# Gathering page keys through copied row lists, with a pause taken out and two sets of rooms

## The chip, the cores and the metric

The kernel runs on one core of one Trainium2 chip. The metric is the device time of one execution in microseconds (us). The core has five instruction queues that run beside each other, each strictly in its own order: TensorE (PE, matmuls; PEld is its loading of weights), VectorE (DVE), ScalarE (ACT), GpSimd (POOL) and SyncE (SP, which only issues DMA transfers here). POOL issues the indirect DMA transfers, the gathers.

## The reference, cut to what matters

One decoder layer for 1024 prompt tokens and for 8 sequences of 4 new tokens. The part that the change touches is the attention of the new tokens over 8192 past tokens, whose latent keys (256 wide) and rotary keys (64 wide) lie in pages of 128 tokens, found through a page table:

```python
def one_seq(args):
    ql, qr, pt, c_new, r_new = args
    c_past = cache_ckv[pt].reshape(-1, KV_LORA)
    r_past = cache_kr[pt].reshape(-1, MLA_ROPE)
    s_past = jnp.einsum('thc,kc->htk', ql, c_past) + jnp.einsum('thr,kr->htk', qr, r_past)
    ...
    p = jax.nn.softmax(sc, axis=-1).astype(c_new.dtype)
    return (jnp.einsum('htk,kc->thc', p[..., :n_past], c_past)
            + jnp.einsum('htk,kc->thc', p[..., n_past:], c_new))
```

Beside it the layer has input projections (x times w_in, in many columns), a retention branch, the attention of the prompt, gates and output projections. All values are float32.

## The kernel before, in words

**Matmuls in parts.** The projections split each float32 operand in a high and a low half and run three matmuls for each product (lines 266 to 268, helper mac). Each weight tile is loaded by SP, cast by ACT (line 247) and its low half taken by DVE (line 198). One weight tile of a gate or value column serves 72 matmuls of 128x352.

**Fill.** The columns of w_in that belong to gates and to the retention values are computed by a generator called `fill`, which gives way after each product. Three stages consume it, each through `beside(main, total, fill, budget)`: after each step of the stage's own work, which yields a cost, as many products of fill are issued as the budget allows in proportion. What is left of fill runs by itself at the end (`run(fill)`, line 717). The yields of the stage thus set how many fill matmuls stand between its steps.

**Page attention** (lines 576 to 703). The eight sequences go in two groups g of four. In each group the 64 pages of a sequence go in eight steps jj of eight pages. One pair (g, jj), a unit, is one run of `past_keys`: sixteen units in all, here numbered 0 to 15. Of a unit:

- `gather` issues, for each of four sequences s and each of two blocks i, one indirect DMA of the rotary keys (128 rows of 1 KB, line 584, tile rraw) and one of the latent keys (128 rows of 4 KB, line 585, tile craw). The row numbers lie in the columns of `idx`, worked out once before (`page_rows`).
- Five steps n make scores. Step 0 takes the rotary keys, steps 1 to 4 take 64 columns each of the latent keys. In each, DVE turns the keys of the four sequences (line 634, tile kt, a ring of 8, so two steps' worth), and PE runs 32 score matmuls (line 640).
- DVE takes the maximum (line 645, nb), ACT the exponentials (line 652), PE turns the probabilities (line 661), DVE and ACT copy them out (line 662), PE multiplies them with the latent keys (line 667, pv), and DVE adds that to the running sum (line 669, acc).

The tile craw has 8 rooms, two units' worth; rraw has 2 rooms of two sequences each, one unit's worth. A tile's new writer waits for all readers of the room's last content.

**Order.** A scheduler in the tile layer puts the instructions on each engine's queue: it follows the program, but lets an instruction that it takes to be ready earlier go ahead of others. So the order on DVE is not that of the source: the turned rotary keys of the next unit, for one, stand ahead of the maximum of this one. What stands in a queue behind a waiting instruction waits too.

Of the kernel before, what the change touches and what calls it, by code (L numbers as in the profile page):

```python
# [9 lines left out]
F32 = mybir.dt.float32  # L10
F32R = mybir.dt.float32r
BF16 = mybir.dt.bfloat16
I32 = mybir.dt.int32
# [6 lines left out]
P = 128  # L20
# [4 lines left out]
NR = NB * NS  # L25
# [4 lines left out]
NPG = PAST // PAGE  # L30
# [3 lines left out]
HM = 8  # L34
NOPE = 128
ROPE = 64
QL = 384
KL = 256
# [122 lines left out]
def decode_step(ctx: ExitStack, tc: tile.TileContext, A: dict, O: dict):  # L161
    nc = tc.nc
    pe, act, dve, pool, sp = nc.tensor, nc.scalar, nc.vector, nc.gpsimd, nc.sync
# [207 lines left out]
    idx = lp.tile([P, NB * NPG // 4], I32, name="idx")  # L371
# [102 lines left out]
    p3 = ph.enter_context(tc.tile_pool(name="p3", bufs=1))  # L474
    NSEQ, NJ, NK = 4, 10, 2

    def big(name, shape, rows_=P):
        return p3.tile([rows_, *shape], F32, tag="craw", name=name, bufs=2 * NSEQ)

    def mid(name, shape):  # L480
        return p3.tile([P, *shape], F32, tag="mid", name=name, bufs=2)
# [14 lines left out]
    def sample_queries():  # L496
        pt = tr()
        for i in range(5):
            pe.transpose(pt[:, i * NR:(i + 1) * NR], latS[:, i * P:(i + 1) * P], ident[:NR, :NR])
        pe.transpose(pt[:ROPE, 5 * NR:6 * NR], latS[:, QL + KL:], ident[:NR, :NR])  # L500
        cqT = p3.tile([P, 3, NR], F32, name="cqT")
        dve.tensor_copy(cqT, pt[:, :3 * NR].rearrange("p (a b) -> p a b", a=3))
        dve.tensor_copy(kvST, pt[:, 3 * NR:5 * NR].rearrange("p (a b) -> p a b", a=2))
        dve.tensor_copy(krST, pt[:ROPE, 5 * NR:6 * NR])
        wq = [big("wq", (3, 384)) for _ in range(4)]
        for c in range(4):
            sp.dma_start(wq[c], A["w_uq"][0, :, c * 384:(c + 1) * 384].rearrange("(k p) f -> p k f", p=P))
        wk = big("wk", (2, HM, NOPE))
        for c in range(2):
            sp.dma_start(wk[:, c], A["w_ukv"][0, c * P:(c + 1) * P, :].rearrange("p (h d) -> p h d", h=HM)[:, :, :NOPE])  # L510
        yield 6.0
        qs = big("qq", (1536,))[:NR].rearrange("p (h d) -> p h d", h=HM)
        qq = big("qq", (768,))
        qr = qq[:NR, :512].rearrange("p (h d) -> p h d", h=HM)
        qnT = qq[:, 512:768].rearrange("p (h r) -> p h r", h=HM)
        ps = mm()
        for k in range(3):
            for c in range(4):
                pe.matmul(ps[c * NR:(c + 1) * NR, :384], cqT[:, k, :], wq[c][:, k], start=k == 0,
                          stop=k == 2, tile_position=(0, c * NR), skip_group_check=True)  # L520
        yield 2.0
        for c in range(4):
            act.activation(qs[:, 2 * c:2 * c + 2, :].rearrange("p h d -> p (h d)"), ps[c * NR:(c + 1) * NR, :384], AF.Copy, scale=MSC)  # L523
            yield 0.5
        for c in range(2):
            rope_nat(qr[:, 4 * c:4 * c + 4, :], qs[:, 4 * c:4 * c + 4, NOPE:], 8, NR, p3, 4, "qro")
            yield 1.0
        pt = tr()
        for h in range(HM):
            pe.transpose(pt[:, h * NR:(h + 1) * NR], qs[:, h, :NOPE], ident[:NR, :NR])  # L530
        act.copy(qnT, pt[:, :HM * NR].rearrange("p (h r) -> p h r", h=HM))
        yield 1.0
        wkT = big("wkT", (HM, KL))
        for h in range(HM):
            pt = tr()
            for c in range(2):
                pe.transpose(pt[:, c * P:(c + 1) * P], wk[:, c, h, :], ident)
            (act.copy if h % 2 else dve.tensor_copy)(wkT[:, h, :], pt[:, :KL])
            yield 0.5
        qlT = Q["qlT"] = ring("qlT", (2, NB, 32))  # L540
        pl = mm()
        for c in range(2):
            for h in range(HM):
                o = (c * HM + h) * NR
                pe.matmul(pl[:, o:o + NR], wkT[:, h, c * P:(c + 1) * P], qnT[:, h, :], start=True, stop=True)
            dve.tensor_copy(qlT[:, c].rearrange("p b (h t) -> p h b t", t=NS),
                            pl[:, c * HM * NR:(c + 1) * HM * NR].rearrange("p (h b t) -> p h b t", h=HM, b=NB))
            yield 2.0
        pt = tr()
        for h in range(HM):  # L550
            pe.transpose(pt[:ROPE, h * NR:(h + 1) * NR], qr[:, h, :], ident[:NR, :NR])
        dve.tensor_copy(qrT.rearrange("p b (h t) -> p h b t", t=NS), pt[:ROPE, :HM * NR].rearrange("p (h b t) -> p h b t", h=HM, b=NB))
        sel = ring("sel", (4, 4, 32))
        dve.tensor_copy(sel, ident.rearrange("p (q r) -> p q r", q=4).unsqueeze(2).to_broadcast([P, 4, 4, 32]))
        sel = sel.rearrange("p q g r -> p q (g r)")
        q4 = q4_tile()
        other = [ring("q4b", (w, NSEQ, 32)) for w in (4, 4, 2)]
        for n in range(5):
            px = tr()
            for i in range(2):  # L560
                j = 2 * n + i
                o = px[:, i * 256:(i + 1) * 256]
                if j < 8:
                    pe.matmul(o, sel[:, j % 4], qlT[:, j // 4].rearrange("p b r -> p (b r)"), start=True, stop=True)
                else:
                    pe.matmul(o, sel[:ROPE, i], qrT.rearrange("p b r -> p (b r)"), start=True, stop=True)
            src = px.rearrange("p (i g s r) -> p i g s r", i=2, g=2, s=NSEQ)
            dve.tensor_copy(q4[:, 2 * n:2 * n + 2], src[:, :, 0])
            act.copy(other[n // 2][:, 2 * (n % 2):2 * (n % 2) + 2], src[:, :, 1])
            yield 1.0  # L570
        for n, o in enumerate(other):
            w = 4 if n < 2 else 2
            sp.dma_start(q4D[:, 4 * n:4 * n + w], o)
        Q["q4"] = q4
# [1 line left out]
    rows_c = A["cache_ckv"].rearrange("l n (s a) c -> (l n s) (a c)", a=4)  # L576
    rows_r = A["cache_krope"].rearrange("l n (s a) c -> (l n s) (a c)", a=4)

    def gather(b, jj, c, r):

        for i in range(NK):
            at_ = b * (NPG // 4) + NK * jj + i
            off = bass.IndirectOffsetOnAxis(ap=idx[:, at_:at_ + 1], axis=0)
            pool.indirect_dma_start(out=r[:, i], out_offset=None, in_=rows_r, in_offset=off)  # L584
            pool.indirect_dma_start(out=c[:, i], out_offset=None, in_=rows_c, in_offset=off)  # L585

    def new_tokens(g, st):

# [20 lines left out]
        act.copy(acc, pv[:, :KL])  # L609
        yield 1.0  # L610

    def past_keys(g, jj, st):

        seqs = [4 * g + s for s in range(NSEQ)]
        rr = [p3.tile([P, 2, NK, 4 * ROPE], F32, tag="rr", name="rraw", bufs=2) for _ in range(2)]
        cr = [big("craw", (NK, 4 * KL)) for _ in seqs]  # L620
        for s, b in enumerate(seqs):
            gather(b, jj, cr[s], rr[s // 2][:, s % 2])
        keys = [c.rearrange("p i (a d) -> p (i a) d", a=4) for c in cr]
        rope = [rr[s // 2][:, s % 2].rearrange("p i (a d) -> p (i a) d", a=4) for s in range(NSEQ)]
        yield 6.0
        W = 128 * NK
        sc = psg.tile([P, 4, 512], F32, tag="sc", name="sc", bufs=1)[:, :, :W]
        steps = [8, *range(0, 8, 2)]
        for n, j in enumerate(steps):
            kt = []  # L630
            for s in range(NSEQ):
                t = ring("kt").rearrange("p (j k) -> p j k", j=2)
                src = keys[s][:, :, 32 * j:32 * j + 64] if j < 8 else rope[s]
                dve.transpose(t.rearrange("p j (n r) -> p n j r", r=32), src.rearrange("p n (j r) -> p n j r", r=32))  # L634
                kt.append(t)
            for i in range(2):
                for q in range(4):
                    qs_ = slice(32 * q, 32 * q + 32)
                    for s in range(NSEQ):
                        pe.matmul(sc[32 * s:32 * s + 32, q, :], Q["q4"][qs_, j + i, s, :], kt[s][qs_, i, :], start=n + i == 0,  # L640
                                  stop=n == NJ // 2 - 1 and i == 1, tile_position=(32 * q, 32 * s), skip_group_check=True)
            if n % 2:
                yield 6.0
# [21 lines left out]
        for n in range(4 * NK):  # L665
            for s in range(NSEQ):
                pe.matmul(pv[32 * s:32 * s + 32, :KL], pT[:, n, 32 * s:32 * s + 32], keys[s][:, n, :], start=n == 0, stop=n == 4 * NK - 1,  # L667
                          tile_position=(0, 32 * s), skip_group_check=True)
        dve.scalar_tensor_tensor(out=acc, in0=acc, scalar=corr, in1=pv[:, :KL], op0=ALU.mult, op1=ALU.add)
        yield 1.0  # L670

    def page_attention():
        state = [{}, {}]
        yield from new_tokens(0, state[0])
        for g in range(2):
            if g == 1:
                q4 = q4_tile()
                sp.dma_start(q4, q4D)
                Q["q4"] = q4
                yield from new_tokens(1, state[1])  # L680
            for jj in range(NPG // 4 // NK):
                yield from past_keys(g, jj, state[g])
        olT = ring("olT", (2, HM, NB, NS))
        for g, st in enumerate(state):
            rl = p3.tile([P, 1], F32, tag="rl", name="rl", bufs=2)
# [274 lines left out]
    for h in range(HR):  # L960
        run(head_vg(h, X))
        nxt = {}
# [521 lines left out]
```

## Time and profile before

| | |
|---|---|
| median of 3 runs | 2253.39 us (2249.23 to 2253.68) |
| the profiled execution | 2248.48 us, of it span 2246.7 us |
| PE busy | 2192.1 us |
| DVE busy | 1207.9 us |
| ACT busy | 709.8 us |
| POOL busy | 509.9 us |
| score matmuls (line 640) | from 207.6 to 791 us of the span |
| gathers (lines 584 and 585) | 128 and 128, 123.7 and 120.5 us of POOL |

A row of a timeline gives the start in the span, the duration, the engine, the line and operation, the tiles (out<-in), their shapes, and xN for N instructions merged; in square brackets stands the engine's idle time before the row and what ended it. A score matmul leaves two records. Time to landing is from a transfer's issue to its data's arrival.

### The profile page before, as it was taken

How to read it: one execution, taken by the hardware profiler on the slowest of the kernel's cores; microseconds unless marked ns; L12 is line 12 of the kernel's file. 1: busy time of each engine (PE TensorE's matmuls, PEld its weight loads, DVE VectorE, ACT ScalarE, POOL GpSimd, SP SyncE). 2: the span in 40 equal slices, each digit the busy share in tenths (PEclk: the TensorE clock that was granted, in tenths of full speed). 3: DMA queues.
4: the chain of work that ended last, by engine and by line, in shares of the span. 5: the costliest groups of instructions: out<-in, count | busy, mean ns of one | idle time of the engine just before them, and what ended most of it. 6: DMA issues, size and time to landing. Idle time of an engine off the chain costs nothing.

```text
span 2246.7 us, 45040 instructions
## 1 busy us (share of the span) xinstructions
PE 2192.1 (98%) x18482; PEld 1975.0 (88%) x18482; DVE 1207.9 (54%) x2624; ACT 709.8 (32%) x1532; POOL 509.9 (23%) x682
## 2 busy tenths in 40 slices
PE   8899999999999999999999999999999999999997
PEld 7898888888888899798798779888887999999997
DVE  5414454444544438728638447767767344454465
ACT  6312112222322123222222122355456332222243
POOL 2224434344444114203203102122222000000021
PEclk9999999999999999999999999999999999999999
DMA  8446565656565442532613753200110453333243
GB/s 234 131 148 247 184 223 174 227 183 222 182 232 178 153 135 59 165 99 66 212 49 95 237 162 87 81 23 24 37 46 27 149 192 106 96 94 107 87 141 114
DMA packets 293391, 303.65 MB, mean 135 GB/s; under 512 B 29760, under 2 KB 242048, under 8 KB 293184
## 3 DMA queue, kind: packets, MB, share of 16 engines
q1 hardware_dynamic: 268608, 216.86, 31.3%
q0 software_dynamic: 24576, 83.90, 10.8%
q8 instruction: 145, 2.38, 0.4%
q14 instruction: 62, 0.51, 0.1%
HBM read 234.76 MB, written 65.94 MB: 134 GB/s over the span
## 4 chain that ended last, share of the span: by engine, by line
PE 82%; DVE 7%; issue 6%; POOL 3%; ACT 2%; DMA 1%; SPq 0%; POOLq 0%; ACTq 0%; DVEq 0%
PE mm L266 19%; PE mm L268 18%; PE mm L267 18%; PE sc L640 5%; PE x L667 3%; PE mm L1199 2%; PE ac L267 2%; PE ac L268 2%; PE ac L266 2%; PE tr L1186 1%; PE ac L936 1%; PE ac L932 1%; DVE Stl L198 1%; PE ac L1139 1%; PE tr L791 1%
## 5 line engine op out<-in xcount | busy, mean ns | idle before, releaser
L266 PE MATMUL mm<-xh,wh 128*128 128x352 f32 x1728 | 577.4, 334 | 0.2 <-ACT qq L523 0.2
L268 PE MATMUL mm<-xh,wl 128*128 128x352 f32 x1728 | 562.4, 325 | 0.0
L267 PE MATMUL mm<-xl,wh 128*128 128x352 f32 x1728 | 560.5, 324 | 0.0
L266 PEld LDWEIGHTS mm<-xh,wh 128*128 128x128 f32 x1728 | 324.6, 188 | 38.4 <-issue 29.5
L268 PEld LDWEIGHTS mm<-xh,wl 128*128 128x128 f32 x1728 | 325.5, 188 | 18.6 <-issue 17.3
L267 PEld LDWEIGHTS mm<-xl,wh 128*128 128x128 f32 x1728 | 325.8, 189 | 14.5 <-issue 7.2
L198 DVE TENSOR_TENSOR wl<-wr,wh 128x512 fp32r<-128x512 f32 (+2 forms) x283 | 189.0, 679 | 202.4 <-ACT wh L247 175.7
L247 ACT CAST wh<-wr 128x512 fp32r<-128x512 f32 x248 | 149.8, 619 | 356.0 <-PE mm L267 319.2
L634 DVE STREAM_TRANSPOSE kt<-craw 128x512 f32<-128x512 f32 x256 | 159.3, 679 | 151.0 <-PE sc L640 150.4
L413 ACT ACTIVATE gev<-mm 128x352 f32<-128x352 f32 x132 | 61.1, 463 | 357.2 <-PE mm L268 256.7
L584 POOL DMA_INDIRECT rraw<-in_cache_krope_dram,idx x128 | 123.7, 966 | 215.4 <-DVE kt L634 166.2
L585 POOL DMA_INDIRECT craw<-in_cache_ckv_dram,idx x128 | 120.5, 941 | 142.6 <-PE x L667 102.2
L640 PE MATMUL sc<-kt,q 32*32 32x256 f32 x5120 | 125.5, 385 | 0.1
L266 PE MATMUL mm<-mh,wh 128*128 128x352 f32 x384 | 124.3, 324 | 0.8 <-DVE M L1309 0.8
L267 PE MATMUL mm<-ml,wh 128*128 128x352 f32 x384 | 124.5, 324 | 0.0
L268 PE MATMUL mm<-gh,wl 128*128 128x352 f32 x384 | 124.3, 324 | 0.0
L266 PE MATMUL mm<-gh,wh 128*128 128x352 f32 x384 | 124.3, 324 | 0.0
L268 PE MATMUL mm<-mh,wl 128*128 128x352 f32 x384 | 124.2, 324 | 0.0
L267 PE MATMUL mm<-gl,wh 128*128 128x352 f32 x384 | 124.1, 323 | 0.0
L1415 POOL TENSOR_TENSOR xr<-x1h,x1l 128x352 f32<-128x352 f32 x24 | 26.1, 1106 | 404.7 <-PE mm L268 367.0
L640 PEld LDWEIGHTS sc<-kt,q 32*32 32x32 f32 x5120 | 75.1, 103 | 34.0 <-issue 9.5
L1164 POOL TENSOR_SCALAR pr<-pr,rl 128x896 f32<-128x896 f32 (+3 forms) x64 | 49.7, 777 | 133.3 <-DVE rl L1163 91.0
(351 smaller groups left out, 4294.4 us busy)
## 6 DMA issues: line engine op xcount, KB each, us to landing
wr<-in_w_in_dram SPq DMA_DIRECT2D x144, 256.0 KB, 3.6
st<-in_state_ret_dram SPq DMA_DIRECT2D x32, 512.0 KB, 5.2
out_ret_sample_dram<-st SPq DMA_DIRECT2D x32, 512.0 KB, 3.3
wr<-in_w_ple_gate_dram SPq DMA_DIRECT2D x48, 256.0 KB, 3.0
gt<-gev SPq DMA_DIRECT2D x48, 176.0 KB, 3.3
gl<-go SPq DMA_DIRECT2D x16, 528.0 KB, 4.2
gate<-ga SPq DMA_DIRECT2D x16, 528.0 KB, 3.5
g<-gt SPq DMA_DIRECT2D x32, 256.0 KB, 3.2
```

The source lines that it names most:

```text
L198: dve.tensor_tensor(out=out, in0=src, in1=b32(hi), op=ALU.subtract)
L247: hi_by[0](hi, raw)
L266: pe.matmul(out, wh, xh, start=first, stop=False)
L267: pe.matmul(out, wh, xl, start=False, stop=False)
L268: pe.matmul(out, wl, xh, start=False, stop=last)
L413: act.activation(t, ps, func)
L584: pool.indirect_dma_start(out=r[:, i], out_offset=None, in_=rows_r, in_offset=off)
L585: pool.indirect_dma_start(out=c[:, i], out_offset=None, in_=rows_c, in_offset=off)
L634: dve.transpose(t.rearrange("p j (n r) -> p n j r", r=32), src.rearrange("p n (j r) -> p n j r", r=32))
L640: pe.matmul(sc[32 * s:32 * s + 32, q, :], Q["q4"][qs_, j + i, s, :], kt[s][qs_, i, :], start=n + i == 0, stop=n == NJ // 2 - 1 and i == 1, ...
L667: pe.matmul(pv[32 * s:32 * s + 32, :KL], pT[:, n, 32 * s:32 * s + 32], keys[s][:, n, :], start=n == 0, stop=n == 4 * NK - 1, tile_position ...
L1164: pool.tensor_scalar(p_[:, :W], p_[:, :W], rl, 1.0, op0=ALU.mult, op1=ALU.mult)
```

## The change

The gathers leave `past_keys`. A new `keys_of` takes the tiles of a unit, craw from one of two tags by the parity of jj (four rooms each, instead of one tag of eight). `gather` now serves one sequence: DVE copies its two row numbers from idx into a small tile `rows` (a ring of four), and the two rotary and two latent gathers take their offsets from that copy. Unit 0 is gathered ahead of `new_tokens`; each later unit is gathered in the unit before it, one sequence in each of the steps 1 to 4. The `yield 6.0` at the head of `past_keys` goes with the gathers. The tiles that the query stage keeps in these rooms are put to one of the two tags by hand.

```diff
-    def big(name, shape, rows_=P):
-        return p3.tile([rows_, *shape], F32, tag="craw", name=name, bufs=2 * NSEQ)
+    def big(name, shape, side=0):
+        return p3.tile([P, *shape], F32, tag=f"craw{side}", name=name, bufs=NSEQ)
...
-    def gather(b, jj, c, r):
-        for i in range(NK):
-            at_ = b * (NPG // 4) + NK * jj + i
-            off = bass.IndirectOffsetOnAxis(ap=idx[:, at_:at_ + 1], axis=0)
-            pool.indirect_dma_start(out=r[:, i], out_offset=None, in_=rows_r, in_offset=off)
-            pool.indirect_dma_start(out=c[:, i], out_offset=None, in_=rows_c, in_offset=off)
+    def keys_of(g, jj):
+        rr = [p3.tile([P, 2, NK, 4 * ROPE], F32, tag="rr", name="rraw", bufs=2) for _ in range(2)]
+        cr = [big("craw", (NK, 4 * KL), jj % 2) for _ in range(NSEQ)]
+        return g, jj, cr, rr
+
+    def gather(keys, s):
+        g, jj, cr, rr = keys
+        at_ = (4 * g + s) * (NPG // 4) + NK * jj
+        rows_ = p3.tile([P, NK], I32, tag="rows", name="rows", bufs=4)
+        dve.tensor_copy(rows_, idx[:, at_:at_ + NK])
+        for out, src in ((rr[s // 2][:, s % 2], rows_r), (cr[s], rows_c)):
+            for i in range(NK):
+                off = bass.IndirectOffsetOnAxis(ap=rows_[:, i:i + 1], axis=0)
+                pool.indirect_dma_start(out=out[:, i], out_offset=None, in_=src, in_offset=off)
...
-    def past_keys(g, jj, st):
-        seqs = [4 * g + s for s in range(NSEQ)]
-        rr = [p3.tile([P, 2, NK, 4 * ROPE], F32, tag="rr", name="rraw", bufs=2) for _ in range(2)]
-        cr = [big("craw", (NK, 4 * KL)) for _ in seqs]
-        for s, b in enumerate(seqs):
-            gather(b, jj, cr[s], rr[s // 2][:, s % 2])
+    def past_keys(now, nxt, st):
+        _, _, cr, rr = now
...
-        yield 6.0
+        coming = None
...
+            if n and nxt:
+                if coming is None:
+                    coming = keys_of(*nxt)
+                gather(coming, n - 1)
             for i in range(2):
...
+        st["keys"] = coming
         yield 1.0
...
     def page_attention():
         state = [{}, {}]
+        units = [(g, jj) for g in range(2) for jj in range(NPG // 4 // NK)]
+        keys = keys_of(*units[0])
+        for s in range(NSEQ):
+            gather(keys, s)
         yield from new_tokens(0, state[0])
...
-                yield from past_keys(g, jj, state[g])
+                yield from past_keys(keys, dict(zip(units, units[1:])).get((g, jj)), state[g])
+                keys = state[g]["keys"]
```

The two integers that the copies hold are the same row numbers as before; no arithmetic changes.

More of the change, by code (lines that the diff above doesn't have):

```diff
@@ L507, in sample_queries @@
             sp.dma_start(wq[c], A["w_uq"][0, :, c * 384:(c + 1) * 384].rearrange("(k p) f -> p k f", p=P))
-        wk = big("wk", (2, HM, NOPE))
+        wk = big("wk", (2, HM, NOPE), 1)
         for c in range(2):
@@ L511, in sample_queries @@
         yield 6.0
-        qs = big("qq", (1536,))[:NR].rearrange("p (h d) -> p h d", h=HM)
-        qq = big("qq", (768,))
+        qs = big("qq", (1536,), 1)[:NR].rearrange("p (h d) -> p h d", h=HM)
+        qq = big("qq", (768,), 1)
         qr = qq[:NR, :512].rearrange("p (h d) -> p h d", h=HM)
@@ L532, in sample_queries @@
         yield 1.0
-        wkT = big("wkT", (HM, KL))
+        wkT = big("wkT", (HM, KL), 1)
         for h in range(HM):
```

## The prediction

> **What bounds the kernel now.** I read the page's busy times first, then busy time by stretch, then the engines' timelines through one unit of the page attention (a unit: eight pages of each of four sequences).
>
> ```profile
> PE 2192.1 (98%) x18482; PEld 1975.0 (88%) x18482; DVE 1207.9 (54%) x2624; ACT 709.8 (32%) x1532; POOL 509.9 (23%) x682
> ...
> PE 82%; DVE 7%; issue 6%; POOL 3%; ACT 2%; DMA 1%; SPq 0%; POOLq 0%; ACTq 0%; DVEq 0%
> ```
>
> ```profile
> 200.00:800.00 600.00, 599.95 (x8691) 508.30 (x8690) 280.78 (x474) 142.03 (x260) 222.31 (x234) 1.00 0.58 191
> ```
>
> ```profile
> 806.00:846.00 40.00, 40.00 (x249) 40.00 (x249) 17.30 (x28) 8.47 (x18) 10.61 (x11) 1.00 0.52 167
> ```
>
> The columns of the stretches are length, then PE, PEld, DVE, ACT, POOL busy, granted clock, DMA share, GB/s. The change lies inside 200 to 800. There PE is busy 599.95 of 600 us: it runs score and value matmuls of the pages and, between them, gate matmuls ("fill"). PE waits for nothing there, so the change has nothing to win unless it removes PE work, and it removes none. It can only open holes.
>
> One unit on PE (its pv ends, and the fill starts, at 467.67; I call this moment T0):
>
> ```profile
> 467.67 0.43 PE L266 MATMUL mm<-xh,wh 128*128 128x352 f32 x1
> ...
> 473.70 1.91 PE L640 MATMUL sc<-kt,q 32*32 32x256 f32 x70
> ...
> 476.06 1.61 PE L640 MATMUL sc<-kt,q 32*32 32x256 f32 x58
> ...
> 482.81 1.91 PE L640 MATMUL sc<-kt,q 32*32 32x256 f32 x70
> ...
> 485.17 1.45 PE L640 MATMUL sc<-kt,q 32*32 32x256 f32 x58
> ...
> 491.77 1.68 PE L640 MATMUL sc<-kt,q 32*32 32x256 f32 x64
> ...
> 505.79 0.42 PE L266 MATMUL mm<-xh,wh 128*128 128x352 f32 x1
> ```
>
> Steps 0 and 1 of the scores take from 473.70 to 477.67, 3.97 us; steps 2 and 3 from 482.81 to 486.62, 3.81; step 4 1.68. Two fill matmuls stand within each pair. Ahead of 473.70 the built order has 36 fill matmuls: 6.03 us, 0.168 each. The unit is 38.1 us long.
>
> The gathers of the next unit, on POOL, and on DVE the instruction that ends the unit (L669) and the next transposes:
>
> ```profile
> 468.00 0.94 POOL L585 DMA_INDIRECT craw<-in_cache_ckv_dram,idx  x1 [7.39 <-PE x L667]
> ...
> 471.74 0.94 POOL L585 DMA_INDIRECT craw<-in_cache_ckv_dram,idx  x1 [0.30 <-issue]
> ...
> 476.86 0.94 POOL L585 DMA_INDIRECT craw<-in_cache_ckv_dram,idx  x1 [0.30 <-issue]
> ```
>
> ```profile
> 457.22 0.13 DVE L648 TENSOR_TENSOR nm<-nm,nb 128x1 f32<-128x1 f32 x1
> ...
> 467.89 0.48 DVE L669 SCALAR_TENSOR_TENSOR acc<-acc,corr,x 128x256 f32<-128x256 f32 x1 [4.89 <-PE x L667]
> ...
> 475.29 4.86 DVE L634 STREAM_TRANSPOSE kt<-craw 128x512 f32<-128x512 f32 x8
> ```
>
> Times to landing (least, median, most): of the ckv gathers of this unit from the second on, of all ckv gathers between 210 and 790, and of the krope gathers there.
>
> ```profile
> DMA to landing us min/median/max: 8.2/8.2/8.4
> ```
>
> ```profile
> DMA to landing us min/median/max: 4.3/7.9/9.0
> ```
>
> ```profile
> DMA to landing us min/median/max: 2.6/2.8/6.2
> ```
>
> So the before already gathers a unit ahead: the eight ckv gathers of unit u+1 start 0.3 us after T0 of unit u, when pv of u-1 has let their room go, one every 1.25 us, and with 8.0 us each have landed by T0+17. Their first reader on DVE stands after the scores of u, and nothing waits for them.
>
> **The change part by part.**
>
> *Rooms and order of gathers.* The two tags hold four tiles each, by parity of jj; one tag of eight went round in the same way. In the built program POOL's order from unit 2 on is unchanged: eight krope gathers of a unit, then its eight ckv gathers, 1.25 us apart, ckv behind pv of two units before. Cost nothing; the issue row at 468.00 stays the model. SP's queue holds the same loads.
>
> *Fill.* The pause of 6.0 at the head of each unit goes, so after pv only 3 to 6 fill matmuls stand instead of 36 to 39, and 735 instead of 259 follow the last unit. 476 matmuls move; in the stretch 806:846 they run 249 in 40.00 us, 0.161 each, as in the units. Moved work, no gain and no loss, if nothing was hidden under it. It hid something: 30 x 0.165 = 5 us per unit, in which DVE and the gathers ran ahead.
>
> *Row lists.* 64 copies on DVE of two integers; 60 of them stand behind waits. One costs between the 0.13 us of the smallest DVE instruction shown (L648) and the 0.48 of L669, whose tile is 128 times as wide; I take 0.15, nearest in size. Their work, under 10 us, lies beside PE. Their wait does not. The ring has four lists, so list s of unit u+2 may be written only when list s of u+1 is read out, and the built program makes the copy wait for the completion counts of the two ckv gathers that used it: it waits for landing, not issue. And the copies stand a unit earlier than the source reads. DVE's order after L669 (c, R: transposes of ckv, krope; r: copies for u+2; w: lo halves of fill weights; NB: the maximum):
>
> ```
> units 1-7:  c | c c c r0 r1 c | c c c r2 r3 c | c c c c | R R R R | NB
> units 9-13: c c c c r0 r1 | c c c c r2 r3 | c c c c | R R R R | NB
> ```
>
> In units 1-7 the first c ends step 1, then come steps 2, 3, 4; in 9-13 steps 2, 3, 4 follow at once. Behind a waiting copy all later transposes of DVE are queued, PE waits for them, and behind PE everything else.
>
> *Units 1-7.* The last ckv gather of u+1 is issued at T0+9.2 (476.86 - 467.67). With 8.0 us it lands at T0+17.2; r3 then costs 0.15, the last transpose of step 3 0.61 (4.86/8): T0+17.95. PE then has 29 matmuls of step 3 left, 1.6: done at T0+19.55. Without the wait PE would be there at 1.0 (6 fill) + 3.97 + 4.9 (30 fill) + 3.8 = T0+13.65. A hole of 5.9 us; seven units, 41. In unit 7 two lo halves, in unit 4 one, stand between r3 and the transpose: 2 more. 43.
>
> *Units 9-13.* Here the pairs have no fill within:
>
> ```profile
> 626.96 2.81 PE L640 MATMUL sc<-kt,q 32*32 32x256 f32 x128
> ```
>
> Step 3's transposes wait for r1: the fourth gather is issued at T0+4.1, landed at 12.1; two copies 0.3, four transposes 2.45, then 1.4 of matmul: T0+16.2. Unhindered: 1.0 + 2.81 + 5.4 (33 fill) + 2.81 = T0+12.0. Hole 4.2; r2 and r3 then end at 17.5, early enough for step 4. Five units: 21. Unit 8, with r0 and r1 before step 2 and some 18 more fill, by the same sum 3.7. Units 14 and 15 copy nothing: 0.
>
> *Unit 0.* Its four copies (for unit 2) stand before the last transpose of step 1 and wait for unit 1's krope gathers, which wait for unit 0's first transposes:
>
> ```profile
> 199.30 0.95 POOL L584 DMA_INDIRECT rraw<-in_cache_krope_dram,idx  x1 [9.88 <-DVE kt L634]
> ...
> 207.96 0.95 POOL L584 DMA_INDIRECT rraw<-in_cache_krope_dram,idx  x1 [0.30 <-issue]
> ```
>
> ```profile
> 207.56 1.91 PE L640 MATMUL sc<-kt,q 32*32 32x256 f32 x70
> ...
> 210.04 1.67 PE L640 MATMUL sc<-kt,q 32*32 32x256 f32 x58
> ```
>
> All eight in a row go out by 209, land 2.8 later, copy and transpose: 212.6. PE, with 30 fill less ahead, begins at 202.7 and wants that transpose at 205.2. Hole 7.
>
> *Before unit 0.* The copies for unit 1 stand among the wkT copies and wait for unit 0's ckv gathers:
>
> ```profile
> 169.24 0.94 POOL L585 DMA_INDIRECT craw<-in_cache_ckv_dram,idx  x1 [0.30 <-issue]
> ```
>
> ```profile
> 174.80 0.42 DVE L538 COPY wkT<-tr 128x256 f32<-128x256 f32 x1 [1.90 <-PE tr L537]
> ```
>
> 169.24 + 8 = 177.2 against 174.80: 2.4 late, less what three transpose banks cover; between 0 and 2.4, I take 1.
>
> **Sum.** 43 + 21 + 3.7 + 7 + 1 = 76 us. The profiled execution took 2248.48 (span 2246.7); 2248.5 + 76 = 2324.5. The median of the runs is 4.9 above that execution; I put the forecast at 2326.
>
> The one size that matters is the landing: 13 holes move with it. At the 6.9 of the quickest steady units the sum is 62, at the 9.0 of the slowest 89: 2312 to 2339.
>
> **Rivals.**
>
> *Quick landing.* If a gather took the least shown, 4.3 us, r3 would be released at T0+13.5; the holes are 2.2 in units 1-7 and 0.4 in 9-13, with unit 0 some 27 us: 2276. Against it: 8.2/8.2/8.4 in the steady unit, where gathers follow each other every 1.25 us. Chance 0.15. [...]
>
> *Paced one unit ahead.* If the copies did what the source reads, timing unit u+1's gathers inside u, no list would hold DVE, but gathers would start at T0+4.5, and ckv of the third sequence land near T0+29.7, just behind the need of the probabilities' copy on DVE: 1 us in 15 units, 2264. The built order speaks against it. Chance 0.04.
>
> *Not slower.* If a list were free once its gather is issued rather than landed, r3 would come at T0+10.1 and all transposes ahead of PE; PE would stay full: 2248 to 2254. It decides at a landing of 2.1 us (13.65 - 1.6 - 0.76 - 9.2); even krope gathers, a quarter as large, take 2.6. Chance 0.06, half of it on either side of faster and same.
>
> *Longer chain.* The holes also hold back DVE's lo halves and ACT's exp; if the fill's weights run late too, or gathers land in over 9 us, another 10 to 35: 2335 to 2360. For it: the lo halves stand right behind copies in four units. Against: a weight is split 72 fill matmuls (11.6 us) before use. Chance 0.13.
>
> **How the numbers follow.** The forecast as summed, 2312 to 2339, has 0.62. The range 2278 to 2350 takes it, most of the quick landing and of the longer chain, and leaves out some 0.2. A measurement here tells about 0.2%, 4.5 us; slower than that: 0.94, same 0.03, faster 0.03.
>
> **What would show it.** Right: between 200 and 800 PE idles some 70 us, put down to DVE's transposes (line 640); DVE waits at line 590 for DMAs of craw, 4 to 6 us a unit in longest pieces; the gather rows stay 1.25 us apart, starting with pv's end; the first half's units idle more than the second's. Wrong: PE busy in the units as now, or holes elsewhere (probabilities, fill), or landings far from 8 us.

## The result, and the profile after

The changed kernel takes 2341.59 us (median of 4 runs, 2341.03 to 2348.04), the kernel before beside it 2253.14 (2249.23 to 2253.68). The ratio is 1.0403, with an interval from 1.0381 to 1.0425: 88 us slower, where 2326 was forecast. The profiled execution took 2341.38, of it span 2339.5, which is 92.8 more than the 2246.7 of before.

The page of the changed kernel, busy times and the chain that ended last:

```profile
PE 2237.3 (96%) x18482; PEld 1995.3 (85%) x18482; DVE 1219.2 (52%) x2688; ACT 709.8 (30%) x1532; POOL 509.5 (22%) x682
...
PE 72%; DMA 8%; DVE 7%; issue 7%; POOL 4%; ACT 2%; SPq 0%; POOLq 0%; ACTq 0%; DVEq 0%
```

DMA has 8% of the chain where it had 1. PE runs the same 18482 matmuls, yet is busy 45.2 us longer (2237.3 against 2192.1). So of the 92.8 us only 47.6 are idle time of PE; the other half stands in the column "busy". That is the first thing that the prediction does not explain. The stretches (length, PE, PEld, DVE, ACT, POOL busy, granted clock, DMA share, GB/s) show where:

```profile
200.00:520.00 320.00, 278.76 (x3927) 215.62 (x3937) 139.71 (x257) 48.71 (x98) 117.42 (x123) 0.90 0.50 163
520.00:800.00 280.00, 274.34 (x4183) 223.03 (x4184) 138.70 (x253) 71.43 (x119) 103.88 (x110) 0.98 0.57 189
800.00:850.00 50.00, 49.73 (x353) 47.62 (x352) 9.00 (x19) 13.56 (x25) 0.00 (x0) 0.97 0.42 130
```

PE idles 41.2 us of the first 320 and 5.7 of the next 280, and its granted clock, 1.00 between 200 and 800 before, is 0.90 and 0.98. The moved fill, in the tail behind 800, runs at its old pace (249 matmuls in the 40 us from 840 to 880), but for one dip of the clock, to which the last section comes back.

The waits of DVE between 150 and 900 (total us, times, longest), and those of PE's weight loads up to 900:

```profile
DVE rows L590 <- DMA craw<-in_cache_ckv_dram,rows: 107.6, 55, 4.2
...
DVE rows L590 <- DMA rraw<-in_cache_krope_dram,rows: 7.1, 3, 4.7
```

```profile
PEld sc L650 <- DVE kt L640: 69.5, 60, 8.1
```

The copies wait for the landing of latent gathers, 55 times. PE waits for the transposes behind them. Now one unit, in which pv ends and fill starts at 451.97 (T0). POOL's first and last latent gather of the next unit:

```profile
452.30 0.94 POOL L594 DMA_INDIRECT craw<-in_cache_ckv_dram,rows  x1 [7.51 <-PE x L677]
...
461.00 0.94 POOL L594 DMA_INDIRECT craw<-in_cache_ckv_dram,rows  x1 [0.30 <-issue]
```

DVE in the same unit, from the end of one unit to the end of the next:

```profile
452.19 0.48 DVE L679 SCALAR_TENSOR_TENSOR acc<-acc,corr,x 128x256 f32<-128x256 f32 x1 [5.39 <-PE x L677]
...
458.91 0.17 DVE L590 COPY rows<-idx 128x2 int32<-128x2 int32 x1 [2.06 <-DMA craw<-in_cache_ckv_dram,rows]
462.37 0.17 DVE L590 COPY rows<-idx 128x2 int32<-128x2 int32 x1 [3.29 <-DMA craw<-in_cache_ckv_dram,rows]
462.47 2.49 DVE L640 STREAM_TRANSPOSE kt<-craw 128x512 f32<-128x512 f32 x4
...
469.02 0.17 DVE L590 COPY rows<-idx 128x2 int32<-128x2 int32 x1 [2.29 <-DMA craw<-in_cache_ckv_dram,rows]
469.12 2.49 DVE L640 STREAM_TRANSPOSE kt<-craw 128x512 f32<-128x512 f32 x4
...
492.72 0.48 DVE L679 SCALAR_TENSOR_TENSOR acc<-acc,corr,x 128x256 f32<-128x256 f32 x1 [3.69 <-PE x L677]
```

And PE:

```profile
463.24 2.39 PE L650 MATMUL sc<-kt,q 32*32 32x256 f32 x64 [0.67 <-DVE kt L640]
465.56 0.43 PE L266 MATMUL mm<-xh,wh 128*128 128x352 f32 x1
465.83 0.32 PE L267 MATMUL mm<-xl,wh 128*128 128x352 f32 x1
469.89 2.33 PE L650 MATMUL sc<-kt,q 32*32 32x256 f32 x58 [3.75 <-DVE kt L640]
472.15 0.66 PE L268 MATMUL mm<-xh,wl 128*128 128x352 f32 x1
472.61 0.49 PE L266 MATMUL mm<-xh,wh 128*128 128x352 f32 x1
...
475.17 0.32 PE L266 MATMUL mm<-xh,wh 128*128 128x352 f32 x1
```

Read the three together. The eighth gather is issued at 461.00; the last copy is let go when it has landed, 8.0 us later; the transposes of step 3 follow, and PE, with nothing to do since 466.15, begins 0.9 us behind that copy. That is the predicted hole, and PE stands still for 3.75 us of it. What was not predicted comes behind it: 58 records of score matmuls take 2.33 us where 58 took 1.45 before, and fill matmuls last 0.49 instead of 0.32 for three microseconds more. The granted clock, in stretches of 2 us, says why:

```profile
466.00:468.00 2.00, 0.14 (x1) 0.00 (x0) 0.30 (x2) 0.00 (x0) 0.00 (x0) 1.00 0.90 310
468.00:470.00 2.00, 0.11 (x15) 0.11 (x26) 0.98 (x3) 0.00 (x0) 0.00 (x0) 0.55 0.73 225
470.00:472.00 2.00, 2.00 (x58) 0.88 (x58) 1.61 (x3) 0.00 (x0) 0.00 (x0) 0.50 0.09 31
472.00:474.00 2.00, 2.00 (x18) 1.85 (x7) 1.79 (x3) 0.00 (x0) 0.00 (x0) 0.50 0.03 8
474.00:476.00 2.00, 2.00 (x11) 2.00 (x11) 0.70 (x2) 0.00 (x0) 1.32 (x2) 0.74 0.00 0
476.00:478.00 2.00, 2.00 (x14) 1.94 (x12) 0.00 (x0) 0.46 (x1) 1.53 (x2) 1.00 0.47 131
```

In the hole the clock falls to half, and PE works some 5 us at 0.50 before it is back at 1.00. This hole cost PE more than its 3.75 us.

### The profile page after: what moved, and what is told of

It is laid out like the page before. It is cut to its first block, busy times and chain, and to the rows that moved or that the text cites. A ratio compares the mean times of both kernels' runs of the same rounds, so it can differ in the third digit from the quotient of the medians.

```text
span 2339.5 us, 45049 instructions
## 1 busy us (share of the span) xinstructions
PE 2237.3 (96%) x18482; PEld 1995.3 (85%) x18482; DVE 1219.2 (52%) x2688; ACT 709.8 (30%) x1532; POOL 509.5 (22%) x682
## 4 chain that ended last, share of the span: by engine, by line
PE 72%; DMA 8%; DVE 7%; issue 7%; POOL 4%; ACT 2%; SPq 0%; POOLq 0%; ACTq 0%; DVEq 0%
PE mm L266 17%; PE mm L268 16%; PE mm L267 16%; DMA craw<-in_cache_ckv_dram,rows 4%; PE sc L650 4%; PE x L677 2%; PE mm L1215 2%; PE ac L267 1%; PE ac L268 1%; DMA st<-in_state_ret_dram 1%; PE tr L1202 1%; PE ac L266 1%; POOL craw L594 1%; PE ac L952 1%; PE ac L1155 1%
## 5 line engine op out<-in xcount | busy, mean ns | idle before, releaser
L266 PE MATMUL mm<-xh,wh 128*128 128x352 f32 x1728 | 583.8, 338 | 0.5 <-ACT gev L413 0.3
L268 PE MATMUL mm<-xh,wl 128*128 128x352 f32 x1728 | 569.3, 329 | 0.0
L266 PEld LDWEIGHTS mm<-xh,wh 128*128 128x128 f32 x1728 | 330.3, 191 | 40.3 <-issue 30.8
L268 PEld LDWEIGHTS mm<-xh,wl 128*128 128x128 f32 x1728 | 330.9, 192 | 21.8 <-issue 20.5
L267 PEld LDWEIGHTS mm<-xl,wh 128*128 128x128 f32 x1728 | 330.9, 191 | 13.8 <-issue 6.5
L650 PE MATMUL sc<-kt,q 32*32 32x256 f32 x5120 | 153.7, 411 | 46.9 <-DVE kt L640 46.5
L594 POOL DMA_INDIRECT rraw<-in_cache_krope_dram,rows x128 | 124.1, 969 | 242.0 <-DVE kt L640 193.6
L594 POOL DMA_INDIRECT craw<-in_cache_ckv_dram,rows x128 | 120.4, 941 | 133.0 <-PE x L677 93.3
```

What stands on the lines that cost most here:

```text
L266: pe.matmul(out, wh, xh, start=first, stop=False)
L267: pe.matmul(out, wh, xl, start=False, stop=False)
L268: pe.matmul(out, wl, xh, start=False, stop=last)
L594: pool.indirect_dma_start(out=out[:, i], out_offset=None, in_=src, in_offset=off)
```

## The experiments

Three questions: is it the copies or something else in the change; does their wait for landing do it, by standing in DVE's queue; and what does the clock add. Each kernel ran beside the kernel before on the same chip; ratios are against that one.

**Only the pause taken out** (from the kernel before).

```diff
-        yield 6.0
```

> The kernel before with only the pause of 6.0 at the head of each unit taken out, so that 6 fill matmuls instead of 36 stand between two units; no lists. Landing theory: DVE's order has nothing waiting in it, the gathers issue as before and land 17 us after the unit's start where their first reader comes after 21: about 2253 (2248 to 2258). Pause theory: all of the loss, about 2341.

2254.49 us (2251.24 to 2258.53), ratio 1.0009 [0.9999, 1.0018]. Moving the fill costs nothing by itself, while nothing waits.

**The change without the copies**, offsets straight from idx.

```diff
-        rows_ = p3.tile([P, NK], I32, tag="rows", name="rows", bufs=4)
-        dve.tensor_copy(rows_, idx[:, at_:at_ + NK])
...
-                off = bass.IndirectOffsetOnAxis(ap=rows_[:, i:i + 1], axis=0)
+                off = bass.IndirectOffsetOnAxis(ap=idx[:, at_ + i:at_ + i + 1], axis=0)
```

> The changed kernel without the copies: the gathers take their offsets from idx itself; rooms by parity, gathers written a unit ahead, no pause. Landing theory: about 2253 (2248 to 2258), the order on DVE holds no wait for a gather. A theory that the new rooms or the earlier gathers cost something: above 2258.

2254.47 us, ratio 1.0016 [1.0006, 1.0025]. Its waits of PE's weight loads, and its first stretch:

```profile
PEld sc L648 <- DVE kt L638: 5.1, 16, 0.7
```

```profile
200.00:520.00 320.00, 319.10 (x4951) 257.93 (x4950) 168.11 (x287) 68.55 (x132) 145.84 (x152) 1.00 0.63 208
```

PE is full again, at full clock. Rooms, the place of the gathers and the pause together cost 0.16%; some 87 us (2341.59 less 2254.47) come with the 64 copies.

**Only the copies**, put into the kernel before, with its pause and its one tag.

```diff
+        at_ = b * (NPG // 4) + NK * jj
+        rows_ = p3.tile([P, NK], I32, tag="rows", name="rows", bufs=4)
+        dve.tensor_copy(rows_, idx[:, at_:at_ + NK])
...
-            off = bass.IndirectOffsetOnAxis(ap=idx[:, at_:at_ + 1], axis=0)
+            off = bass.IndirectOffsetOnAxis(ap=rows_[:, i:i + 1], axis=0)
```

> The kernel before with one thing of the change: each sequence's two row numbers are copied on DVE into a ring of four lists and the gathers read those; the pause and the one tag of eight rooms stay. Landing theory: the copies for the next but one unit stand right behind the sum L669, the second is free 12 us after it, so step 1's last transposes come at T0+13 and its scores end 4.6 us late in units 1 to 7, 2.3 late in 8 to 13, 3 in unit 0: 49 us, and up to 17 more if PE's clock drops after holes of that length: 2302 to 2320. Pause theory: no loss, 2253.

2302.13 us, ratio 1.0215 [1.0191, 1.0238]: the low end of what the landing theory gave. The parts agree less well than the sum: by the end-of-unit rows, against the kernel before, 36 us are lost in units 1 to 7 (32 expected), 6 in 8 to 13 (14) and 12 up to the end of unit 0 (3). The clock falls here too (0.50 from 438 to 440), and its share, put at up to 17 on top, is in these numbers. So the total is right in part by luck.

**The change with the pause put back**:

```diff
         coming = None
+        yield 6.0
```

> The changed kernel with the pause of 6.0 put back at the head of each unit. Pause theory: about 2253. Landing theory: the order on DVE becomes that of the kernel before with lists alone (two copies right behind the sum), so the same time as that kernel, 2302 to 2320; if PE's 36 fill matmuls covered the wait fully, 2253, which the order speaks against.

2300.94 us, ratio 1.021 [1.0191, 1.0228], 1 us below the range. The two agree: with the pause the copies cost 48 to 50 us, without it 87. The pause theory, which gave 2253 for both, falls. In both, DVE's order is another one: two copies stand right behind the end of the unit, ahead of the last transposes of step 1. What DVE waits for at the copies in the first of the two kernels, and what PE waits behind them in one of its units:

```profile
DVE rows L583 <- DMA craw<-in_cache_ckv_dram,rows: 141.5, 43, 7.2
```

```profile
437.49 2.33 PE L642 MATMUL sc<-kt,q 32*32 32x256 f32 x58 [3.35 <-DVE kt L636]
```

DVE waits longer than in the changed kernel (141.5 us against 107.6), and yet less is lost: in this unit DVE waits 10.1 us at its first two copies, but PE only 3.35, since the fill that the pause puts between pv and the scores runs meanwhile. How long DVE waits is not what it costs here; what PE has in its queue meanwhile decides.

**A ring of eight lists** instead of four.

```diff
-        rows_ = p3.tile([P, NK], I32, tag="rows", name="rows", bufs=4)
+        rows_ = p3.tile([P, NK], I32, tag="rows", name="rows", bufs=8)
```

> The changed kernel with a ring of eight row lists instead of four, all else kept (the pause gone, fill moved, copies on DVE). A list of unit u+2 then waits for the gathers of unit u, landed long before. Landing theory (the copies hold DVE until the last unit's gathers have landed): the holes go, about 2253 us (2248 to 2260). Pause theory (what costs is the 5 us of fill taken from between the units): nothing changes, about 2341. Copy theory (the copies' own work or order costs): about 2341, or a few us less.

2337.75 us (2337.11 to 2342.01), ratio 1.0381 [1.036, 1.0401]: the expectation was wrong. The group of its copies, with that of the changed kernel first (duration min/median/max in ns, first and last start):

```profile
L590 DVE COPY rows<-idx x64: 149/169/416, 156.5 to 728.4; 128x2 int32<-128x2 int32 x64
```

```profile
L590 DVE COPY rows<-idx x64: 150/169/379, 156.2 to 694.1; 128x2 int32<-128x2 int32 x64
...
  DMA craw<-in_cache_ckv_dram,rows: 102.2, 49
```

The last copies, for unit 15, stand in unit 13 with four lists and in unit 12 with eight: the scheduler took the greater freedom to put them a whole unit earlier, and there they wait for the same gathers as before, those in flight. Room alone does not take a wait away where the order follows the room.

**All lists in one tile**, 64 copies into columns of their own, none reused.

```diff
+    lists = p3.tile([P, NB * NPG // 4], I32, name="lists")
...
-        rows_ = p3.tile([P, NK], I32, tag="rows", name="rows", bufs=4)
+        rows_ = lists[:, at_:at_ + NK]
         dve.tensor_copy(rows_, idx[:, at_:at_ + NK])
```

> The changed kernel with the same 64 copies, but each into its own two columns of one tile, so that no copy has to wait for an earlier list to be read out. Landing theory: the copies all run before the first unit, 11 us of DVE beside other work, and the holes go: 2253 (2248 to 2262, if the copies delay the stage before by some us). Copy theory (the cost is the copying, or gathers taking offsets from a copy): about 2340.

2254.81 us, ratio 1.0016 [1.0006, 1.0025]. The same 64 copies on DVE, with nothing to wait for, cost nothing beside the change without copies, which had 1.0016 too: it is the reuse of a list, not the work of copying.

**Half of the copies**: lists for two of the four sequences, a ring of two.

```diff
-        rows_ = p3.tile([P, NK], I32, tag="rows", name="rows", bufs=4)
-        dve.tensor_copy(rows_, idx[:, at_:at_ + NK])
+        rows_ = idx[:, at_:at_ + NK]
+        if s < 2:
+            rows_ = p3.tile([P, NK], I32, tag="rows", name="rows", bufs=2)
+            dve.tensor_copy(rows_, idx[:, at_:at_ + NK])
```

> The changed kernel with lists for the first two sequences of a unit alone, in a ring of two; the other two gathers take their offsets from idx. The last wait on DVE is then the second sequence's, T0+12 instead of T0+17: holes of 3.5 us in units 1 to 7, split in two, 3 to 4 in units 8 to 13, 4 in unit 0. Landing theory: 45 to 50 us, 2295 to 2305; if the clock drops after holes this short too, up to 2315. Any theory by which the number of copies counts: half of 88, about 2297, so time alone does not tell these apart, but where DVE waits and whether the clock stays at 1.00 does.

2301.68 us, ratio 1.0223 [1.0206, 1.024]. With r2 and r3 gone, units 1 to 7 lose 17.3 us against the change without copies (in the change itself 56.7), while units 9 to 13, where r1 alone made the hole, lose 20.9 (19.3): each copy costs where it stands, as the order on DVE says. The clock stays at 1.00 from 264 to 540 us, through units 2 to 7, and the 17.3 lost in units 1 to 7 are less than the 24 that seven holes of 3.5 would make: their second copy starts at T0+10.4 on average, where 12 was expected.

**The same copies on POOL**, in the ring of four, with the same waits.

```diff
-        dve.tensor_copy(rows_, idx[:, at_:at_ + NK])
+        pool.tensor_copy(rows_, idx[:, at_:at_ + NK])
```

> The changed kernel with the same copies into the same ring of four, made by POOL instead of DVE. They wait for the same gathers, but behind them POOL's queue holds only the next unit's gathers, which wait for room anyway, and none of PE's inputs. Landing theory in its full form (the loss is what stands behind the waiting instruction, not the wait): 2253 (2248 to 2260). If the ring of four delays the gathers themselves: above 2270.

2256.24 us (2254.39 to 2258.45), ratio 1.0016 [1.0007, 1.0026]. Two of the copies in its POOL timeline:

```profile
449.60 0.18 POOL L590 COPY rows<-idx 128x2 int32<-128x2 int32 x1 [4.12 <-DMA craw<-in_cache_ckv_dram,rows]
452.52 0.18 POOL L590 COPY rows<-idx 128x2 int32<-128x2 int32 x1 [2.75 <-DMA craw<-in_cache_ckv_dram,rows]
```

They wait for landings too, here 4.12 and 2.75 us and between 440 and 490 six times, 13.4 in all, but only gathers with slack are queued behind them. So the wait cost by what was behind it in DVE's queue, the transposes.

**Keeping PE busy.** The changed kernel with idle work added: 20 matmuls whose result nobody reads, between steps 2 and 3 of units 1 to 7, and 40 ahead of step 1 of unit 0.

```diff
                 gather(coming, n - 1)
+            if now[0] == 0 and (n == 3 if now[1] else n == 1):
+                warm = xb()
+                for _ in range(20 if now[1] else 40):
+                    pe.matmul(warm[:, :TH], xn[0][0][:, :P], xn[0][0][:, :TH], start=True, stop=True)
```

> The changed kernel with work added to PE: in units 1 to 7, 20 matmuls of 128x352 (3.3 us) that nobody reads stand between step 2 and step 3, where the 3.7 us hole is, and in unit 0 40 of them ahead of step 1. The waits stay as they are. Clock theory (part of the loss, about 20 us of the 88, is the granted clock halving for some 6 us after each hole over about 3.5 us): faster than the changed kernel by 12 to 22 us, 2320 to 2330, and the clock near 1.00 in the first half. If the holes alone cost: 2341 to 2346.

2325.14 us (2322.01 to 2329.88), ratio 1.0334 [1.0316, 1.0352]: with 180 matmuls more it is 16.5 us faster than the change. One unit on its PE, and the clock there:

```profile
451.24 3.47 PE L649 MATMUL x<-xh 128*128 128x352 f32 x20
454.64 2.20 PE L654 MATMUL sc<-kt,q 32*32 32x256 f32 x64
...
457.04 0.32 PE L267 MATMUL mm<-xl,wh 128*128 128x352 f32 x1
```

```profile
454.00:456.00 2.00, 1.87 (x44) 1.01 (x43) 1.48 (x4) 0.00 (x0) 0.00 (x0) 1.00 0.83 236
456.00:458.00 2.00, 2.00 (x49) 1.55 (x32) 2.00 (x4) 0.00 (x0) 0.00 (x0) 1.00 0.32 104
```

The idle work fills the hole, the clock stays at 1.00, and fill goes on at 0.32 at once. The 3.5 us in the expectation is no limit: in units 0 to 7 of the change PE has seven waits longer than that, of 3.64 to 7.79 us, each with the clock at 0.50 around or behind it, but the last section has shorter ones with the same fall. Not all of the gain need be the clock's: the last copy of a unit starts, on average of units 1 to 7, 16.2 us behind the end-of-unit row on DVE instead of 17.1, since gathers landed quicker here (median 7.0 us for the latent ones between 210 and 790, 7.3 in the change). Seven times 0.85 is 6 us of the 18 won in these units, the rest, 12, is left for the clock. Why they landed quicker I did not test.

## Why the prediction was right, and where it was not

The sum stage by stage, from the end-of-unit rows of DVE (line 679 of the change, two of which are shown above; sixteen in each kernel). The change without copies is what the kernel would be without holes:

| | change | without copies | lost | predicted | with idle work, lost |
|---|---|---|---|---|---|
| up to the end of unit 0 | 245.79 | 236.90 | 8.9 | 8 | 8.4 |
| units 1 to 7 | 288.68 | 231.98 | 56.7 | 43 | 38.5 |
| unit 8 | 37.75 | 37.43 | 0.3 | 3.7 | 1.4 |
| units 9 to 11 | 102.81 | 94.39 | 8.4 | 12.6 | 7.5 |
| units 12 and 13 | 74.39 | 63.53 | 10.9 | 8.4 | 10.9 |
| units 14 and 15 | 63.34 | 63.31 | 0.0 | 0 | 0.0 |
| in all | | | 85.2 | 76 | 66.6 |

**The mechanism held.** Slower, by lists that are released at landing, with copies waiting in DVE's queue. Removing the copies, their reuse, or their place on DVE each brings the time back to within 0.16%; nothing else in the change does anything of that size. Priced at nothing, and rightly to within 0.16%: rooms, gather order and the moved fill (1.0009 and 1.0016). A copy was put at 0.15 us and takes 0.17. Of the 15.6 us between 2326 and 2341.6, 9.2 are in the table; some 3 come from the base, since 2326 less 76 is 2250 and the kernel before took 2253.1; the rest is about the 0.16%.

**Units 1 to 7: the times held, the price of the hole did not.** The last copy was due at T0+17.2; in the unit shown it starts at T0+17.05 (469.02), on average of the seven at 17.3. Step 3 was to end at T0+19.55 and ends at 20.2 (472.15). The step that failed is "PE then has 29 matmuls of step 3 left, 1.6", and the sum that takes a hole at its length: both run PE at full clock right after it has stood still. Behind the hole the clock is 0.50; the rest of step 3 takes 2.33 us, and fill behind it runs on at half pace. Measured 56.7 against 43: 14 us, 2 in each unit. With the clock kept up by idle work the same units lose 38.5. Quicker landing accounts for 6 us of that gain, and 43 less 6 is 37: the holes alone are about what I had summed.

At the 3.75 us hole above the clock reads 0.55, 0.50, 0.50, 0.74, then 1.00 in stretches of 2 us from 468. The fall comes some 2.1 us into the hole, with 1.00 from 466.16 to 468.20 and 0.51 from there to 469.88; then PE works 5.2 us at half clock, from 469.89 to 475.05. I had forecast fourteen holes of 3.7 to 7 us and priced none of this.

**Units 9 to 13: two misses that cancel.** Predicted 4.2 in each. In units 9 to 11 it is 2.8, because the landing was over-sized there: r1, due at T0+12.1, starts between 10.2 and 11.0. Of all latent gathers between 210 and 790 the times to landing are (least, median, most):

```profile
DMA to landing us min/median/max: 5.7/7.3/8.5
```

against the 8.0 that I took throughout; for the last gather of a unit in units 1 to 7, where it mattered most, 8.0 was right. Units 12 and 13 lose 5.4 each instead. Their r1 starts at T0+12.1 and 11.3, as forecast or earlier, but behind the hole the clock falls there too. PE in units 10 and 12, with the clock behind the hole of 12:

```profile
618.40 3.22 PE L650 MATMUL sc<-kt,q 32*32 32x256 f32 x64 [0.62 <-DVE kt L640]
```

```profile
687.80 3.66 PE L650 MATMUL sc<-kt,q 32*32 32x256 f32 x64 [2.06 <-DVE kt L640]
```

```profile
690.00:692.00 2.00, 2.00 (x56) 1.09 (x28) 0.00 (x0) 0.00 (x0) 0.00 (x0) 0.52 0.32 123
```

**Unit 0 and unit 8.** Unit 0 with what stands ahead of it was to lose 8 and lost 8.9; its hole is here, predicted 7:

```profile
213.80 2.33 PE L650 MATMUL sc<-kt,q 32*32 32x256 f32 x58 [7.79 <-DVE kt L640]
```

For unit 8 I predicted 3.7; nearly nothing was lost. PE comes to its step 2 only at T0+14.8 (549.05), behind the matmuls of the new tokens and the fill that they bring, and the transposes were done by then: I had counted too little fill ahead of it.

**What I said would show it.** Gathers 1.25 us apart from pv's end, DVE's waits at line 590 for craw, the first half idler than the second: all there. DVE's single waits there are shorter than the 4 to 6 us that I named: the longest is 4.2, in the unit shown 3.29. "PE idles some 70 us" did not come: it idles 46.9 between 200 and 800. Part of what I called hole is booked as busy: while PE takes its tiles one transpose at a time, 64 records take 2.39 us at clock 1.00 (row 463.24), and behind the hole it is the half clock.

**The rivals.** Quick landing fell: no latent gather landed in under 5.7 us. Paced, and a list free at issue, fell with DVE's waits at line 590. The longer chain had named 2335 to 2360, and the time lies there, but not for its reasons: no latent gather took over 8.5 us, and fill hardly waited, 0.5 us in all 1728 matmuls of its first row:

```profile
L266 PE MATMUL mm<-xh,wh 128*128 128x352 f32 x1728 | 583.8, 338 | 0.5 <-ACT gev L413 0.3
```

A third cause, the clock, gave about what it had asked for. So the sum's own bounds, 2312 to 2339, missed by 2.6 us, and the wider range, 2278 to 2350, held because it had room for a chain of another kind. That is luck as far as the clock goes.

## What to carry to other kernels

In these programs a list that a gather reads its offsets from is held until that gather has landed. The ring of four turned a copy of 0.17 us into a wait for the end of the transfer's flight (8.0 us from issue to copy in the unit shown), and everything behind it in DVE's queue paid. Put such copies on an engine behind which nothing urgent stands, or give each its own place; a longer ring helps only if the order stays where it was. When you forecast holes on PE, look in a trace for the granted clock behind them and add what a lower one costs: here, at 0.50, some 2 us for each hole of units 1 to 7 that I had put at some 6, an estimate from the 56.7 lost against 43. Test the reading by filling the hole with idle matmuls.

## What the hardware showed that I had not expected

The clock fell not only at the long holes of units 1 to 7 (3.75 us in the unit shown). In unit 13 PE waits 1.50 us, between score matmuls of 32 by 32 tiles that come one transpose at a time, and the clock goes down:

```profile
723.90 4.11 PE L650 MATMUL sc<-kt,q 32*32 32x256 f32 x64 [1.50 <-DVE kt L640]
```

```profile
724.00:726.00 2.00, 2.00 (x22) 0.71 (x38) 1.67 (x4) 0.00 (x0) 0.00 (x0) 0.55 0.96 383
726.00:728.00 2.00, 2.00 (x60) 0.83 (x28) 1.38 (x3) 0.00 (x0) 0.00 (x0) 0.50 0.21 67
```

Waits of 0.62 (row 618.40) and 0.67 us (row 463.24) left the clock at 1.00, and 1.50, 2.06 and 3.75 did not. Nor does the length of a wait alone tell the cases apart: behind 1.18 us in unit 9 (scores from 583.86) it reads 1.00 up to 592, and behind 0.77 in unit 2 (scores from 298.46) 1.00 up to 300.9 and 0.50 from 301 to 302, with the next wait beginning only at 301.59.

Once it fell without a hole in the profile. In the tail of the changed kernel 32 matmuls of 128x32 stand in a row. The profile, whose ends of matmuls are modelled, shows PE busy without a gap, and at 819.80 the clock falls all the same:

```profile
815.59 3.65 PE L717 MATMUL x<-olT,wv 128*128 128x32 f32 x32
```

```profile
815.60:819.80 4.20, 4.20 (x37) 4.20 (x37) 0.00 (x0) 0.37 (x1) 0.00 (x0) 1.00 0.05 15
819.80:823.20 3.40, 3.40 (x14) 3.40 (x13) 0.00 (x0) 0.23 (x1) 0.00 (x0) 0.50 0.84 282
```

The kernel before runs its 32 matmuls of this kind at 1.00 throughout (798 to 812). So a PE that the profile calls busy lost its clock too, and what the clock goes by stays open. It stayed down for 3.4 us here, for 6.8 in the unit shown (468.20 to 475.05) and for 10.2 around the hole of unit 0 (208.80 to 219.04).

And adding 180 useless matmuls made a kernel 16.5 us faster.
